# Seven block products over eight row tiles instead of six, with sums left in PSUM, in an encoder layer's feed-forward stages

## The chip, the cores and the metric

The kernel runs on one core of a Trainium2 chip. The metric is device microseconds of one execution, start to end, as the median of several runs. The engines are called as the profile calls them: PE is the matrix engine (PEld its weight loads), DVE the vector engine, ACT the scalar engine, POOL GpSimd, and SP the engine whose queue issues every transfer of this kernel. SBUF is the on-chip memory, PSUM the eight banks into which PE accumulates; one bank holds 128 x 512 float32 numbers.

## What is computed

One encoder layer over 256 tokens of width 2048, in float32. Every sub-layer stands between two RMS norms.

```python
def _swiglu(u, w_gate, w_up, w_down):
    return (jax.nn.silu(u @ w_gate) * (u @ w_up)) @ w_down
...
f = _swiglu(_rmsnorm(h, ffn1_pre_g[i]), ffn1_w_gate[i], ffn1_w_up[i], ffn1_w_down[i])
h = h + 0.5 * _rmsnorm(f, ffn1_post_g[i])
m = _mixer(_rmsnorm(h, mix_pre_g[i]), w_qkv[i], na_rpb[i], out_g[i], w_o[i])
h = h + _rmsnorm(m, mix_post_g[i])
f = _swiglu(_rmsnorm(h, ffn2_pre_g[i]), ffn2_w_gate[i], ffn2_w_up[i], ffn2_w_down[i])
h = h + 0.5 * _rmsnorm(f, ffn2_post_g[i])
g = jax.nn.sigmoid(_rmsnorm(h, ple_pre_g[i]) @ w_ple_gate[i])
h = h + _rmsnorm(g * (p[i] @ w_ple_proj[i]), ple_post_g[i])
```

The two feed-forward networks (FFN1 and FFN2) have 5632 hidden columns, that is 11 blocks of 512. They, their gate, up and down products, hold most of the work and are what the change is about. The mixer between them is attention; it is left as it is but for where some of its tiles lie.

## The kernel before

**Products in three passes.** A float32 number x is split into a high part (`hi`, in the engine's reduced float32 type) and the rest (`lo`). A product of two 128-row tiles is then three matmuls into the same PSUM bank: high by high, low by high, high by low (lines 102 to 104 of `mac`). One matmul has 128 tokens as its stationary operand and 512 weight columns streaming through, so 256 tokens are two tiles, `t` = 0 and 1, and the 2048 input columns are 16 row tiles of a weight matrix. ACT makes the weights' high part (`wh`, line 75) and DVE the low part (`wl`, line 76) from the float32 rows that a transfer brought (`raw`), two row tiles per instruction. There are six buffers each for `wh` and `wl`, three for `raw`.

**Block products.** For ten of the eleven blocks of each FFN, `pair_product` computes the gate and the up products together. Both token tiles by both matrices, over six of the sixteen row tiles in two halves of three, form a 2 x 2 by 2 x 2 block product, which is done in seven block products instead of eight (Strassen's scheme in Winograd's form). For that it needs sums of token blocks (`sums`, four of them, made once per FFN by `token_sums`), sums of weight blocks (line 186, `raw_b`), and sums of the results. The seven products go in the order a11, s1, s2, s4, s3, a12, a22; the four that go into a bank of their own (`pair_s`, two banks) are copied or added out of PSUM into SBUF tiles with the tag `part`, and eight vector instructions (lines 186, 232, 233) form the four outputs there. The other ten row tiles of both matrices (`rest`) are multiplied the plain way into four more banks (`pair_v`, `pair_z`, `pair_y`, `pair_x`), between the block products. The first block of each FFN goes the plain way as a whole.

**Groups.** `swiglu` walks over `FF_GROUPS`, (3, 3, 3, 2) blocks. For each block it runs the pair, then `silu` on ACT (`gs`, line 413) and the product with up on DVE (line 456), and puts the transpose of the result into the list `later`. `run_later` empties this list at fixed places of the next pair or of the down product, where PE transposes (`tr`, line 276) and ACT and DVE write the split hidden block (`hid_h` line 282, `hid_l` line 283). After each group the down product of its blocks runs in four column blocks of 512 and is added onto `f` (lines 468 and 470). In the last group this is followed by the gain, the squares for the norm and the residual (`residual`), whose first part is issued in `mid()`, ahead of the last three row tiles of the last down product.

**Order.** The code is written in dataflow form; a scheduler orders the instructions of each engine before the run, and each engine then takes its own in that fixed order. Pools give a tile the buffer that came free first. A buffer of a pool is waited for by whoever wants to write it next: a transfer on SP's queue, ACT's `wh`, or PE's first matmul into a bank.

Of the kernel before, what the change touches and what calls it, by code (L numbers as in the profile page):

```python
# [19 lines left out]
DFF = 5632  # L20
PLE = 256
# [5 lines left out]
FF_GROUPS = (3, 3, 3, 2)  # L27
# [6 lines left out]
def encoder_layer(ctx: ExitStack, tc: tile.TileContext, a: dict, out: bass.AP):  # L34
# [55 lines left out]
    def mac(acc, xs, parts, first=False, last=False, low_last=False):  # L90


        if low_last:
            for i, ((xh, xl), (wh, wl)) in enumerate(zip(xs, parts)):
                nc.tensor.matmul(acc, xh, wh, start=first and i == 0, stop=False)
                nc.tensor.matmul(acc, xh, wl, start=False, stop=False)
            for i, ((xh, xl), (wh, wl)) in enumerate(zip(xs, parts)):
                nc.tensor.matmul(acc, xl, wh, start=False, stop=last and i == len(parts) - 1)
            return
        for i, ((xh, xl), (wh, wl)) in enumerate(zip(xs, parts)):  # L100
            lead, tail = first and i == 0, last and i == len(parts) - 1
            nc.tensor.matmul(acc, xh, wh, start=lead, stop=False)  # L102
            nc.tensor.matmul(acc, xl, wh, start=False, stop=False)  # L103
            nc.tensor.matmul(acc, xh, wl, start=False, stop=tail)  # L104
# [5 lines left out]
    later, raw_loads, splits, ffn_pool = [], [], [], [None]  # L110
# [48 lines left out]
    def pair_product(lhs, sums, wa, ca, wb, cb):  # L159

        rows1, rows2 = ([lhs[k] for k in ks] for ks in ((0, 1, 4), (2, 3, 5)))
        a11, a12, a22 = of_tile(rows1, 0), of_tile(rows2, 0), of_tile(rows2, 1)
        s1, s2, s3, s4 = sums
        nk = len(lhs)

        def bank(x):
            if x == "s":
                return ps_o.tile([P, NB], F32, name="pair_s", tag="o")
            return ps_acc.tile([P, NB], F32, name=f"pair_{x}", tag="acc")  # L180

        def part(name):
            return ffn_pool[0].tile([P, NB], F32, name=name, tag="part", bufs=6)

        def add(out_, x, y):
            nc.vector.tensor_tensor(out_, x, y, op=ALU.add)  # L186

        def rest(w, k, n, c, accs_, first=False, last=False):

            parts = load_parts(w, k * P, n, c)  # L190
            for t, acc in accs_:
                mac(acc, of_tile(lhs[k : k + n], t), parts, first=first, last=last)

        def load_blocks(w, c):

            raw = ffn_pool[0].tile([P, 2, 3, NB], F32, name="raw_b", bufs=2)
            for j in range(2):
                rows_ = w[2 * j * P : 2 * (j + 1) * P, c : c + NB]
                raw_loads.append(nc.sync.dma_start(raw[:, j, :2], rows_.rearrange("(k p) n -> p k n", p=P)))
                nc.sync.dma_start(raw[:, j, 2], w[(4 + j) * P : (5 + j) * P, c : c + NB])  # L200
            return raw[:, 0], raw[:, 1]

        def split3(raw):
            return split(raw[:, :2]) + split(raw[:, 2:])

        ra1, ra2 = load_blocks(wa, ca)
        rb1, rb2 = load_blocks(wb, cb)
        x = bank("s")
        mac(x, a11, split3(ra1), first=True, last=True)
        p1 = part("p1")  # L210
        nc.scalar.copy(p1, x)
        add(ra1, ra1, rb1)
        x = bank("s")
        mac(x, s1, split3(ra1), first=True, last=True)
        r5 = part("r5")
        nc.scalar.copy(r5, x)
        v, z = bank("v"), bank("z")
        rest(wb, 8, 4, cb, [(1, v), (0, z)], first=True)
        run_later()
        add(ra1, ra1, rb2)  # L220
        x = bank("s")
        mac(x, s2, split3(ra1), first=True, last=True)
        w_ = part("w")
        add(w_, x, p1)
        mac(z, s4, split3(rb2))
        add(rb2, rb1, rb2)
        rest(wb, 12, 4, cb, [(1, v), (0, z)])
        x = bank("s")
        mac(x, s3, split3(rb2), first=True, last=True)
        v_ = part("v")  # L230
        add(v_, x, w_)
        nc.vector.tensor_tensor(w_, r5, w_, op=ALU.subtract)
        nc.vector.tensor_tensor(r5, r5, v_, op=ALU.subtract)
        y, x = bank("y"), bank("x")
        mac(y, a12, split3(ra2), first=True)
        add(ra1, ra1, ra2)
        rest(wb, 6, 2, cb, [(1, v), (0, z)], last=True)
        add(r5, v, r5)
        add(w_, z, w_)
        mac(x, a22, split3(ra1), first=True)  # L240
        for k, n in ((6, 2), (8, 4), (12, 4)):
            rest(wa, k, n, ca, [(0, y), (1, x)], last=k == 12)
        assert nk == 16
        add(p1, y, p1)
        add(v_, x, v_)
        return (p1, v_), (w_, r5)
# [39 lines left out]
    def token_sums(*parts):  # L286


        n_all = sum(p_[0].shape[1] for p_ in parts)
        hi, lo = (  # L290
            acts.tile([P, 2, 2, n_all, P], F32R, name=f"sums_{x}", tag=f"sums_{x}") for x in "hl"
        )
        k0 = 0
        for a11, a12, a21, a22 in parts:
            n = a11.shape[1]
            y = [work.tile([P, 2, 2, P], F32, name="y_s", tag="sq")[:, :, :n] for _ in range(2)]
            nc.vector.tensor_tensor(y[0][:, 0], a21, a22, op=ALU.subtract)
            nc.vector.tensor_tensor(y[0][:, 1], y[0][:, 0], a11, op=ALU.subtract)
            nc.vector.tensor_tensor(y[1][:, 0], a11, a21, op=ALU.subtract)
            nc.vector.tensor_tensor(y[1][:, 1], a12, y[0][:, 1], op=ALU.add)  # L300
            for i in range(2):
                hi_, lo_ = (x[:, i, :, k0 : k0 + n] for x in (hi, lo))
                nc.scalar.copy(hi_, y[i])
                nc.vector.tensor_tensor(lo_, y[i], hi_.bitcast(F32), op=ALU.subtract)
# [30 lines left out]
    def load_x(k):  # L335
# [3 lines left out]
        if k < 6:  # L339
            xb = ffn_pool[0].tile([P, 2, S], F32, name="xb", tag="part", bufs=6)  # L340
        else:
            xb = work.tile([P, 2, S], F32, name="xb", tag="hg")
# [7 lines left out]
        if k < 6:  # L350
            x_first.append(xb)
# [16 lines left out]
    def residual(fg, ssf, scale, blocks, rs, g, sums=None, y_pool=None):  # L368
# [22 lines left out]
        if sums is not None:  # L391
            b0, b1 = y0[::2], y0[1::2]
            later.append(
                lambda: sums.extend(
                    token_sums(
                        [y[:, i : i + 2] for y in b0 for i in (0, 2)],
                        [y[:, i : i + 1] for y in b1 for i in (0, 1)],
                    )
                )
            )  # L400
# [5 lines left out]
    def swiglu(pool, f, ssf, res, blocks, rs, sums, w_gate, w_up, w_down, g_post):  # L406
# [9 lines left out]
        for gi, ng in enumerate(FF_GROUPS):  # L416
            hid = []
            for nb in range(f0, f0 + ng):
# [4 lines left out]
                else:  # L423
                    gate, up = accs("gate"), accs("up")
                    if rs is None:
# [6 lines left out]
                        def ahead_up(k):  # L432
                            load_h(k)
                            if k == KB:
                                with tc.issue_after(splits[0].ins), tc.issue_after(splits[1].ins):
                                    for i, x in enumerate(x_first):
                                        g = row_g[:, 0, 2 * i : 2 * i + 2].unsqueeze(2).broadcast_to([P, 2, S])
                                        nc.vector.tensor_tensor(x, x, g, op=ALU.mult)
                                    a1, a2, a3 = x_first
                                    half = [slice(t * P, (t + 1) * P) for t in range(NT)]  # L440
                                    sums[:] = token_sums(
                                        [x[:, :, h_] for h_ in half for x in (a1, a2)],
                                        [a3[:, i : i + 1, h_] for h_ in half for i in range(2)],
# [9 lines left out]
                split_ = new_split(pool, "hid", 3)  # L453
                for t in range(NT):
                    y = up[t] if nb > 0 else pool.tile([P, NB], F32, name="hm", tag="part", bufs=6)
                    nc.vector.scalar_tensor_tensor(y, up[t], rs[t], gs[t], op0=ALU.mult, op1=ALU.mult)
# [31 lines left out]
    with tc.tile_pool(name="ffn1", bufs=2) as pool:  # L488
        f = pool.tile([P, NT, D], F32, name="f", bufs=1)
        ssf, u_blocks, u_rs = square_sums(), [], []  # L490
# [11 lines left out]
    with ExitStack() as att:  # L502
# [66 lines left out]
        def attend(qT, kT, v, bias, o_split, g):  # L569

            for t in range(NT):
# [46 lines left out]
                on = work.tile([P, KB, HD], F32, name="on", tag="hg")  # L618
# [39 lines left out]
    lhs = rows(o_blocks)  # L658
    pool2 = mix.enter_context(tc.tile_pool(name="mix_f", bufs=1))
    f = pool2.tile([P, NT, D], F32, name="f")  # L660
# [29 lines left out]
    ffn2 = ctx.enter_context(ExitStack())  # L690
    f_pool = ffn2.enter_context(tc.tile_pool(name="f2", bufs=1, side="right"))
    p_h = work.tile([P, PLE // P, S], F32R, name="p_h", tag="hg")
    p_l = work.tile([P, PLE // P, S], F32R, name="p_l", tag="hg")
    with tc.tile_pool(name="ffn2", bufs=2) as pool:
        pT = pool.tile([P, PLE // P, S], F32, name="pT", tag="part", bufs=6)
# [125 lines left out]
```

## Time and profile before

| | |
|---|---|
| median of 3 runs | 1956.0 us (1953.11 to 1956.64) |
| span of the profiled execution | 1954.7 us |
| PE busy | 1930.9 us, 99% |
| DVE busy | 1417.7 us, 73% |
| ACT busy | 1027.5 us, 53% |
| transfers | 376.95 MB, mean 193 GB/s |

The page gives no time of the profiled execution besides its span, from the first to the last instruction; the median of the runs is 1.3 us longer. Busy time is the union of the recorded times of an engine's instructions. A line of a group of instructions reads: line, engine, operation, output<-inputs, shapes, count | busy us, mean ns of one | idle time of the engine just before them, and what ended it. A line of the timeline reads: start us, duration us, engine, line, operation, names, shapes, count [idle time before <-what ended it]. A line of a window reads: start:end length, then busy us and count of PE, PEld, DVE, ACT and POOL, the granted clock of PE, the share of the transfer engines and GB/s.

### The profile page before, as it was taken

How to read it: one execution, taken by the hardware profiler on the slowest of the kernel's cores; microseconds unless marked ns; L12 is line 12 of the kernel's file. 1: busy time of each engine (PE TensorE's matmuls, PEld its weight loads, DVE VectorE, ACT ScalarE, POOL GpSimd, SP SyncE). 2: the span in 40 equal slices, each digit the busy share in tenths (PEclk: the TensorE clock that was granted, in tenths of full speed). 3: DMA queues.
4: the chain of work that ended last, by engine and by line, in shares of the span. 5: the costliest groups of instructions: out<-in, count | busy, mean ns of one | idle time of the engine just before them, and what ended most of it. 6: DMA issues, size and time to landing. Idle time of an engine off the chain costs nothing.

```text
span 1954.7 us, 23225 instructions
## 1 busy us (share of the span) xinstructions
PE 1930.9 (99%) x8780; PEld 1596.7 (82%) x8780; DVE 1417.7 (73%) x1613; ACT 1027.5 (53%) x1320; POOL 22.2 (1%) x31
## 2 busy tenths in 40 slices
PE   8999999999999999999999999999999999999998
PEld 6888888888888877888888878888888888888786
DVE  6984887589759775656565588748975997587864
ACT  7554565355535555544445466545553555355563
POOL 0000000000000000000000000000000000000000
PEclk9999999999999999999999999999999999999999
DMA  9475447445745646454554555744574547456463
GB/s 367 182 248 183 173 176 262 165 173 183 258 162 174 218 158 210 147 197 132 168 175 172 195 210 176 263 164 173 183 259 162 174 181 277 144 183 215 154 207 113
DMA packets 192224, 376.95 MB, mean 193 GB/s; under 512 B 8304, under 2 KB 11376, under 8 KB 191856
## 3 DMA queue, kind: packets, MB, share of 16 engines
q1 hardware_dynamic: 192112, 375.46, 55.4%
q8 instruction: 69, 1.13, 0.2%
q14 instruction: 43, 0.35, 0.1%
HBM read 373.33 MB, written 2.10 MB: 192 GB/s over the span
## 4 chain that ended last, share of the span: by engine, by line
PE 95%; DVE 2%; DMA 1%; ACT 1%; issue 1%; POOL 0%; SPq 0%; DVEq 0%; POOLq 0%; ACTq 0%
PE down L102 8%; PE down L104 8%; PE down L103 8%; PE pair_z L104 3%; PE pair_x L104 3%; PE pair_y L104 3%; PE pair_y L102 3%; PE pair_x L102 3%; PE pair_z L103 3%; PE pair_x L103 3%; PE pair_y L103 3%; PE pair_z L102 3%; PE pair_s L103 3%; PE pair_s L102 3%; PE pair_s L104 3%; PE pair_v L104 2%
## 5 line engine op out<-in xcount | busy, mean ns | idle before, releaser
L76 DVE TENSOR_TENSOR wl<-raw,wh 128x1024 fp32r<-128x1024 f32 (+1 forms) x573 | 693.0, 1220 | 301.1 <-ACT wh L75 282.2
L75 ACT CAST wh<-raw 128x1024 fp32r<-128x1024 f32 (+1 forms) x573 | 596.1, 1051 | 542.1 <-PE down L103 139.4
L75 ACT CAST wh<-raw_b 128x1024 fp32r<-128x1024 f32 (+1 forms) x280 | 228.4, 837 | 139.9 <-PE pair_x L103 55.4
L76 DVE TENSOR_TENSOR wl<-raw_b,wh 128x1024 fp32r<-128x1024 f32 (+1 forms) x280 | 252.0, 953 | 59.4 <-ACT wh L75 58.5
L102 PE MATMUL down<-wh,hid_h 128*128 128x512 f32 x704 | 274.7, 391 | 0.2
L104 PE MATMUL down<-wl,hid_h 128*128 128x512 f32 x704 | 274.0, 389 | 0.0
L103 PE MATMUL down<-wh,hid_l 128*128 128x512 f32 x704 | 273.9, 389 | 0.0
L102 PEld LDWEIGHTS down<-wh,hid_h 128*128 128x128 f32 x704 | 132.1, 188 | 28.1 <-ACT hid_h L282 1.1
L104 PEld LDWEIGHTS down<-wl,hid_h 128*128 128x128 f32 x704 | 132.1, 188 | 27.5
L103 PEld LDWEIGHTS down<-wh,hid_l 128*128 128x128 f32 x704 | 132.2, 188 | 27.2
L186 DVE TENSOR_TENSOR raw_b<-raw_b 128x1536 f32<-128x1536 f32 x80 | 138.8, 1755 | 1.4
L102 PE MATMUL pair_y<-wh,u_h 128*128 128x512 f32 x260 | 101.1, 389 | 0.0
L103 PE MATMUL pair_y<-wh,u_l 128*128 128x512 f32 x260 | 101.1, 389 | 0.0
L104 PE MATMUL pair_y<-wl,u_h 128*128 128x512 f32 x260 | 101.1, 389 | 0.0
L102 PE MATMUL pair_x<-wh,u_h 128*128 128x512 f32 x260 | 101.1, 389 | 0.0
L103 PE MATMUL pair_x<-wh,u_l 128*128 128x512 f32 x260 | 101.1, 389 | 0.0
L104 PE MATMUL pair_x<-wl,u_h 128*128 128x512 f32 x260 | 101.1, 389 | 0.0
L104 PE MATMUL pair_v<-wl,u_h 128*128 128x512 f32 x200 | 77.9, 390 | 0.1
L104 PE MATMUL pair_z<-wl,u_h 128*128 128x512 f32 x200 | 77.9, 389 | 0.0
L103 PE MATMUL pair_v<-wh,u_l 128*128 128x512 f32 x200 | 77.8, 389 | 0.0
L102 PE MATMUL pair_v<-wh,u_h 128*128 128x512 f32 x200 | 77.8, 389 | 0.0
L103 PE MATMUL pair_z<-wh,u_l 128*128 128x512 f32 x200 | 77.8, 389 | 0.0
(234 smaller groups left out, 3314.2 us busy)
## 6 DMA issues: line engine op xcount, KB each, us to landing
raw<-in_ffn_w_down SPq DMA_DIRECT2D x88, 1024.0 KB, 5.0
raw<-in_ffn_w_up SPq DMA_DIRECT2D x48, 1024.0 KB, 8.7
raw<-in_w_qkv SPq DMA_DIRECT2D x48, 1024.0 KB, 5.1
raw<-in_ffn_w_gate SPq DMA_DIRECT2D x47, 1024.0 KB, 5.2
raw_b<-in_ffn_w_gate SPq DMA_DIRECT2D x40, 512.0 KB, 5.9
raw_b<-in_ffn_w_up SPq DMA_DIRECT2D x40, 512.0 KB, 6.7
raw<-in_w_o SPq DMA_DIRECT2D x16, 1024.0 KB, 4.9
raw<-in_w_ple_gate SPq DMA_DIRECT2D x16, 1024.0 KB, 5.0
```

What stands on the lines that cost most here:

```text
L75: nc.scalar.copy(wh[:, :n], raw),
L76: nc.vector.tensor_tensor(wl[:, :n], raw, wh[:, :n].bitcast(F32), op=ALU.subtract),
L102: nc.tensor.matmul(acc, xh, wh, start=lead, stop=False)
L103: nc.tensor.matmul(acc, xl, wh, start=False, stop=False)
L104: nc.tensor.matmul(acc, xh, wl, start=False, stop=tail)
L186: nc.vector.tensor_tensor(out_, x, y, op=ALU.add)
```

## The change

The block products now take eight row tiles in two halves of four. All weights of a pair are then split in units of two row tiles. Three of the seven products (a11, then s2, s3 and a22) go one after the other into the same bank `g1` without clearing it: its value is copied or used after each of the first three, and the next product is added onto it. The up outputs go likewise through `u0`. Thus four PSUM banks are used instead of six, three results are copied out by ACT instead of two, four vector instructions form the outputs instead of eight, and `gate` of token tile 1 is read by `silu` straight from PSUM. The groups become (2, 2, 2, 2, 2, 1), with the two buffers per hidden part that this needs instead of three; the group of one block empties the list `later` before its down product. Tiles move: the token sums into the FFN pools, `part` has four buffers instead of six, `raw_b` has four of four row tiles instead of two of six, and some small tiles change pool. `skip_group_check` on the matmuls only silences a check when the program is built.

```diff
+FF_GROUPS = (2, 2, 2, 2, 2, 1)
-FF_GROUPS = (3, 3, 3, 2)
...
     def pair_product(lhs, sums, wa, ca, wb, cb):
-        rows1, rows2 = ([lhs[k] for k in ks] for ks in ((0, 1, 4), (2, 3, 5)))
-        a11, a12, a22 = of_tile(rows1, 0), of_tile(rows2, 0), of_tile(rows2, 1)
+        k1, k2 = slice(0, KB), slice(KB, 2 * KB)
+        a11, a12, a22 = of_tile(lhs[k1], 0), of_tile(lhs[k2], 0), of_tile(lhs[k2], 1)
...
+        def bank(name):
+            return ps_acc.tile([P, NB], F32, name=f"pair_{name}", tag="acc")
+        def kept(name, x):
+            t = ffn_pool[0].tile([P, NB], F32, name=name, tag="part", bufs=4)
+            nc.scalar.copy(t, x)
+            return t
+        def blocks(w, k, c):
+            raw = ffn_pool[0].tile([P, KB, NB], F32, name="raw_b", bufs=4)
+            rows_ = w[k * P : (k + KB) * P, c : c + NB]
+            raw_loads.append(nc.sync.dma_start(raw, rows_.rearrange("(k p) n -> p k n", p=P)))
+            return raw
...
+        ra1, rb1 = blocks(wa, 0, ca), blocks(wb, 0, cb)
+        rb2 = blocks(wb, KB, cb)
+        g1, u0 = bank("g1"), bank("u0")
+        mac(g1, a11, split4(ra1), first=True, last=True)
+        g0_ = kept("g0_s", g1)
         add(ra1, ra1, rb1)
+        mac(u0, s1, split4(ra1), first=True, last=True)
+        u1_ = kept("u1_s", u0)
         run_later()
         add(ra1, ra1, rb2)
+        mac(g1, s2, split4(ra1), last=True)
+        u0_ = kept("u0_s", g1)
+        u1 = bank("u1")
+        rest(wb, 2 * KB, cb, [(1, u1, True), (0, u0, False)])
+        mac(u0, s4, split4(rb2))
         add(rb2, rb1, rb2)
+        ra2 = blocks(wa, KB, ca)
+        rest(wb, 3 * KB, cb, [(1, u1, False), (0, u0, False)], last=True)
+        add(u0_, u0, u0_, ALU.subtract)
+        mac(g1, s3, split4(rb2), last=True)
+        add(u1_, u1_, g1, ALU.subtract)
+        add(u1_, u1, u1_)
+        g0 = bank("g0")
+        mac(g0, a12, split4(ra2), first=True)
         add(ra1, ra1, ra2)
+        mac(g1, a22, split4(ra1))
+        for k in (2 * KB, 3 * KB):
+            rest(wa, k, ca, [(0, g0, False), (1, g1, False)], last=k == 3 * KB)
+        add(g0_, g0, g0_)
+        return (g0_, g1), (u0_, u1_)
...
-                split_ = new_split(pool, "hid", 3)
+                split_ = new_split(pool, "hid", 2)
...
             hrows = rows(hid)
+            if ng == 1:
+                run_later()
             for b in range(D // NB):
-                gp = gain(pool, g_post, b * NB, "g_post", "part", 6) if last else None
+                gp = gain(pool, g_post, b * NB, "g_post", "part", 4) if last else None
```

`token_sums` is called with two parts of two row tiles each per half instead of one of two and one of one, and at the start of FFN1 four pieces of x instead of three are scaled for it. The mixer's `f` and the second set of sums lie in a pool `f2` that is opened before the mixer's output product.

More of the change, by code (lines that the diff above doesn't have):

```diff
@@ L108, in of_tile @@
         return [(hi[:, tok], lo[:, tok]) for hi, lo in lhs]
-    later, raw_loads, splits, ffn_pool = [], [], [], [None]
+    later, raw_loads, splits, ffn_pool, sums_pool = [], [], [], [None], [None]
     def product(
@@ L182, in part @@
[L182 to L201, printed above, removed]
@@ L203, in split3 @@
-        def split3(raw):
-            return split(raw[:, :2]) + split(raw[:, 2:])
[L206 to L211, printed above, removed]
-        add(ra1, ra1, rb1)
[L213 to L217, printed above, removed]
@@ new lines, in split4, with add, rest @@
+        def split4(raw):
+            return split(raw[:, :2]) + split(raw[:, 2:])
+        def add(out_, x, y, op=ALU.add):
+            nc.vector.tensor_tensor(out_, x, y, op=op)
+        def rest(w, k, c, accs_, last=False):
+            parts = load_parts(w, k * P, KB, c)
+            for t, acc, lead in accs_:
+                mac(acc, of_tile(lhs[k : k + KB], t), parts, first=lead, last=last)
+        ra1, rb1 = blocks(wa, 0, ca), blocks(wb, 0, cb)
+        rb2 = blocks(wb, KB, cb)
+        g1, u0 = bank("g1"), bank("u0")
@@ L229, in pair_product @@
[L229 to L235, printed above, removed]
-        add(ra1, ra1, ra2)
[L237 to L242, printed above, removed]
@@ L290, in token_sums @@
         hi, lo = (
-            acts.tile([P, 2, 2, n_all, P], F32R, name=f"sums_{x}", tag=f"sums_{x}") for x in "hl"
+            sums_pool[0].tile([P, 2, 2, n_all, P], F32R, name=f"sums_{x}", tag=f"sums_{x}", bufs=1) for x in "hl"
         )
@@ L349, in load_x @@
             )
-        if k < 6:
+        if k < 2 * KB:
             x_first.append(xb)
@@ L391, in residual @@
         if sums is not None:
-            b0, b1 = y0[::2], y0[1::2]
             later.append(
[L394 to L399, printed above, removed]
+                lambda: sums.extend(token_sums(*([y[:, i : i + 2] for y in y0] for i in (0, 2))))
             )
@@ L452, in swiglu @@
                         gs = [gated(gate[t], t) for t in range(NT)]
-                split_ = new_split(pool, "hid", 3)
+                split_ = new_split(pool, "hid", 2)
                 for t in range(NT):
-                    y = up[t] if nb > 0 else pool.tile([P, NB], F32, name="hm", tag="part", bufs=6)
+                    y = up[t] if nb > 0 else pool.tile([P, NB], F32, name="hm", tag="part", bufs=4)
                     nc.vector.scalar_tensor_tensor(y, up[t], rs[t], gs[t], op0=ALU.mult, op1=ALU.mult)
@@ L687, in encoder_layer @@
     mix.close()
[L690 to L693, printed above, removed]
+    p_h = f_pool.tile([P, PLE // P, S], F32R, name="p_h")
+    p_l = f_pool.tile([P, PLE // P, S], F32R, name="p_l")
     with tc.tile_pool(name="ffn2", bufs=2) as pool:
-        pT = pool.tile([P, PLE // P, S], F32, name="pT", tag="part", bufs=6)
+        pT = pool.tile([P, PLE // P, S], F32, name="pT", tag="part", bufs=4)
         nc.sync.dma_start(pT, a["pT"].rearrange("(k p) s -> p k s", p=P))
```

41 lines of the change are left out of this document (13 added, 28 removed).

## The prediction, made before the changed kernel was run

> **What bounds the kernel now.** I read the page's busy lines and its slices first, then the timeline of PE, then windows cut at the pairs and the down products, and last the groups and waits of one pair.
>
> ```profile
> span 1954.7 us, 23225 instructions
> ...
> PE 1930.9 (99%) x8780; PEld 1596.7 (82%) x8780; DVE 1417.7 (73%) x1613; ACT 1027.5 (53%) x1320; POOL 22.2 (1%) x31
> ...
> PEclk9999999999999999999999999999999999999999
> ```
>
> PE is never idle for long and its clock is granted in full; all its gaps together are 1954.7 - 1930.9 = 23.8 us. What one matmul costs is read from the starts, since the records overlap:
>
> ```profile
> 672.00 0.39 PE L102 MATMUL pair_x<-wh,u_h 128*128 128x512 f32 x1
> 672.23 0.39 PE L103 MATMUL pair_x<-wh,u_l 128*128 128x512 f32 x1
> 672.45 0.39 PE L104 MATMUL pair_x<-wl,u_h 128*128 128x512 f32 x1
> ```
>
> A matmul is recorded with 0.39 us, but the next one starts 0.227 us later. The windows bear this out (first a pair without transposes, then one with eight, a down product of three blocks, and FFN1's last down product of two):
>
> ```profile
> 204.03:245.51 41.48, 41.48 (x185) 34.35 (x183) 36.26 (x37) 23.20 (x28) 0.00 (x0) 1.00 0.58 203
> 245.51:287.88 42.37, 42.37 (x192) 35.17 (x191) 38.14 (x41) 24.61 (x31) 0.00 (x0) 1.00 0.55 199
> ...
> 330.25:396.43 66.18, 66.18 (x298) 54.88 (x296) 37.60 (x37) 26.15 (x27) 0.00 (x0) 1.00 0.51 175
> 672.68:718.94 46.26, 46.04 (x210) 37.52 (x209) 32.54 (x41) 23.46 (x34) 0.55 (x1) 1.00 0.55 182
> ```
>
> 183 weight loads in 41.48 us are 0.2267 us each: the pair runs at PE's pace with no gap at all. DVE is busy 38.14 of 42.37 us (90%) in a full pair, against 57% in a down product. So PE is the bound, with DVE close behind it in the pairs alone.
>
> **What the change removes: three matmuls a pair.** Before: seven products x 3 row tiles x 3 passes = 63, and ten plain row tiles x 2 matrices x 2 token tiles x 3 = 120: 183, the count above. After: 7 x 4 x 3 = 84 and 8 x 2 x 2 x 3 = 96: 180. Twenty pairs save 60 matmuls; 60 x 0.2267 = **13.6 us**, wholly on the path. By the recorded 0.39 us it would be 23 us. [...]
>
> **What it adds to DVE and ACT in a pair.** From the groups of the pair at 245.51, DVE and then ACT:
>
> ```profile
> L76 DVE TENSOR_TENSOR wl<-raw,wh 128x1024 fp32r<-128x1024 f32 x10 | 12.1, 1219 | 1.6 <-ACT wh L75 1.6
> L76 DVE TENSOR_TENSOR wl<-raw_b,wh 128x1024 fp32r<-128x1024 f32 x7 | 8.5, 1221 | 1.8 <-ACT wh L75 1.8
> L186 DVE TENSOR_TENSOR raw_b<-raw_b 128x1536 f32<-128x1536 f32 x4 | 6.9, 1755 | 0.1
> L76 DVE TENSOR_TENSOR wl<-raw_b,wh 128x512 fp32r<-128x512 f32 x7 | 4.8, 685 | 0.0
> ...
> L186 DVE TENSOR_TENSOR v<-pair_x,v 128x512 f32<-128x512 f32 x1 | 0.7, 684 | 0.0
> ```
>
> ```profile
> L75 ACT CAST wh<-raw_b 128x1024 fp32r<-128x1024 f32 x7 | 7.4, 1054 | 4.8 <-PE pair_x L103 3.5 <-PE pair_z L103 0.8 <-ACT hid_h L282 0.3
> L75 ACT CAST wh<-raw_b 128x512 fp32r<-128x512 f32 x7 | 4.3, 621 | 2.0 <-PE pair_x L103 1.7 <-PE pair_s L103 0.3
> ...
> L216 ACT COPY r<-pair_s 128x512 f32<-128x512 f32 x1 | 0.6, 582 | 0.0
> ```
>
> DVE now: 17 x 1.22 + 7 x 0.685 = 25.5 for the splits, 4 x 1.755 = 7.0 for the weight sums, 8 x 0.684 = 5.5 for the outputs: 38.0 us. After: 22 splits x 1.22 = 26.8; four weight sums over 2048 columns, at 1.755 + (1.755 - 0.684) / 2 = 2.29 us each by the step from 512 to 1536 columns, 9.2; four outputs, 2.7: 38.7 us. So DVE gains 0.7 us a pair and reaches 38.8 of 41.7 us, 93%. ACT: 17 x 1.05 + 7 x 0.62 + 2 x 0.58 = 23.4 becomes 22 x 1.05 + 3 x 0.58 = 24.8, at about 26 of 41.7 us. I cost both at nothing, because the waits of this pair show slack:
>
> ```profile
> ACT wh L75 <- PE pair_z L103: 5.6, 5, 3.1
> ACT wh L75 <- PE pair_x L103: 5.2, 3, 3.5
> DVE wl L76 <- ACT wh L75: 3.4, 4, 1.6
> ```
>
> ACT waits for PE to give back `wh` buffers, 10.8 us in a pair, and DVE for ACT: the splits run ahead of PE as far as six buffers allow. The cover is DVE's 4.2 us of idle time a pair, of which 1.4 us go (0.7 of work, 0.7 of PE time); if it were gone, each further DVE microsecond would be one of the span's. Groups of two give DVE a down product after two pairs instead of three.
>
> **What it adds as waits inside a pair.** `g1` is read and then added onto, which no bank of the kernel before is. PE's next product into it waits for the reader. After a11 and s2 the reader is an ACT copy (0.58 us), with s1's 12 x 0.2267 = 2.7 us, and much more, between. After s3 it is one DVE subtraction (0.68 us) with only a12's 2.7 us between. Cost: nothing if DVE comes to it within 2.0 us; if it has to finish a weight sum (2.29) and a split (1.22) first, 2.29 + 1.22 + 0.68 - 2.72 = 1.5 us a pair, 29 us in all. Below nothing it can't be, since PE has no gap here. I take nothing, nearer to the rows above where DVE waits for others. [...] Between pairs I see no wait: the pool gives the bank that came free first, so the next `g1` is the old `u0`, and `silu` reading the old `g1` delays only what needs the fourth bank. SP issues four transfers of 1 MB for the blocks instead of eight smaller ones, and the bytes are the same; `ra2` now comes after others on SP's queue but is needed late. Next pair's `ra1` takes `rb1`'s buffer, free in mid-pair.
>
> **What it adds at the groups' ends.** A group of two has its second block's transposes after the first half of the first down step:
>
> ```profile
> 678.56 0.60 PE L276 MATMUL tr<-ident,r 128*128 128x128 f32 x4
> 678.92 0.48 PE L102 MATMUL down<-wh,hid_h 128*128 128x512 f32 x1
> 679.23 0.40 PE L103 MATMUL down<-wh,hid_l 128*128 128x512 f32 x1
> 679.73 0.50 PE L102 MATMUL down<-wh,hid_h 128*128 128x512 f32 x1
> ```
>
> Here PE lost 0.50 - 0.23 = 0.27 us. There are two such starts now and ten after: 8 x 0.27 = **2.2 us** (0 to 5, if ACT is later). The group of one has nothing to do but wait. What leads to its first down matmul is seen at the end of FFN1's last pair, whose last matmul starts at 672.45, on ACT and on DVE:
>
> ```profile
> 672.71 1.06 ACT L75 CAST wh<-raw 128x1024 fp32r<-128x1024 f32 x1 [0.15 <-PE pair_x L103]
> 674.45 0.73 ACT L413 ACTIVATE gs<-v,r 128x512 f32<-128x512 f32 x1 [0.68 <-DVE v L186]
> ```
>
> ```profile
> 673.73 0.68 DVE L186 TENSOR_TENSOR v<-pair_x,v 128x512 f32<-128x512 f32 x1
> 674.33 1.21 DVE L76 TENSOR_TENSOR wl<-raw,wh 128x1024 fp32r<-128x1024 f32 x1
> 675.46 0.74 DVE L456 SCALAR_TENSOR_TENSOR r<-r,r,gs 128x512 f32<-128x512 f32 x1
> ```
>
> After: matmuls end at about 672.9; the cast that stands first on ACT ends at 673.8; silu 0.73, product 0.74, then transposes at about 675.3; PE has idled from 672.7 but for tile 0's transposes, 0.5 us. That is 2.1 us, less what PE may put in between; without the cast, 1.3. I take **2.0** for each FFN, 4.0 (2.6 to 5.4).
>
> **What it takes from the tail of an FFN.** The last down product's tail needs cover for the norm:
>
> ```profile
> 711.85 0.39 PE L104 MATMUL down<-wl,hid_h 128*128 128x512 f32 x1
> ...
> 715.25 0.39 PE L104 MATMUL down<-wl,hid_h 128*128 128x512 f32 x1
> 715.67 1.34 PE L276 MATMUL tr<-ident,h 128*128 128x128 f32 x8
> ```
>
> Tile 0 ends at 711.85; PE runs 15 of tile 1's 24 matmuls, and the residual's first transposes come just as these end. With one block tile 1 has 12 in all: PE has 12 x 0.2267 = 2.7 us less to do while DVE's chain runs. Either the whole 2.7 us shows, or nothing, if tile 1's own chain starts as much earlier. I take half, **1.4** for each FFN, 2.8 (0 to 5.4). In this product DVE has, for each 5.44 us of PE (24 matmuls), two splits and four instructions of 0.68: 5.2 us. It keeps up but no more. The gains wait on SP for `part` buffers, ahead of weights.
>
> **Elsewhere.** Adding onto `f` happens five times instead of three per column block and FFN: 32 more DVE instructions of 0.68, in down products where DVE is 57% busy: hidden. The token sums grow (rows of FFN1's start):
>
> ```profile
> L438 DVE TENSOR_TENSOR xb<-xb,row_g 128x512 f32<-128x512 f32 x3 | 1.9, 686 | 0.0
> L304 DVE TENSOR_TENSOR sums_l<-y_s,sums_h 128x512 fp32r<-128x512 f32 x2 | 1.3, 689 | 0.2 <-ACT sums_h L303 0.2
> L304 DVE TENSOR_TENSOR sums_l<-y_s,sums_h 128x256 fp32r<-128x256 f32 x2 | 0.8, 418 | 0.0
> ...
> L299 DVE TENSOR_TENSOR y_s<-xb 128x256 f32<-128x256 f32 x1 | 0.4, 418 | 0.0
> L299 DVE TENSOR_TENSOR y_s<-xb 128x128 f32<-128x128 f32 x1 | 0.3, 285 | 0.0
> ```
>
> One `xb` (0.69), 2 x 0.27 and 4 x 0.13: 1.8 us of DVE in FFN1 and 1.1 in FFN2, ahead of a plain up product; I take **0.3** (0 to 2.9). Tiles that only change pool cost nothing unless a transfer waits for the new place.
>
> **The sum**, against the profiled execution: -13.6 + 2.2 + 4.0 + 2.8 + 0.3 = -4.3 us, so a span of 1950.4 us; against the median, 1.3 us longer than that span, **1951.7 us**. With all edges low it is -13.6 + 2.6 = -11.0 (1945.0), with all high -13.6 + 5 + 5.4 + 5.4 + 2.9 = +5.1 (1961.1).
>
> **Rivals.** (1) The edges are nearly free, because PE's order is filled with other ready work: about -10 us, 1946. For it speaks that PE lost only 0.27 us at 679; against it, that one block leaves nothing else ready. (2) Slower: DVE comes late to the subtraction after s3. The point is 8.2 / 20 = 0.41 us a pair, from which the time is 3.9 us above before; at half of the worst price, 0.75 us, it is 15 us, 1966.7. For it speaks DVE's 93% and its two weight sums close to each other there; against it, the waits above, all of them on PE's buffers. (3) The products are saved but the wait and the edges just eat it: 0.2 us a pair more, 1955.7, no change.
>
> **How the numbers follow.** Differences under 0.2%, 3.9 us, are about what this measurement can't tell from none. The main case has 0.58, its own range 1947 to 1956; about six parts in ten of it lie below 1952.1. Rival 1 has 0.13, rival 2 0.20, rival 3 0.09. Faster: 0.35 + 0.13 = 0.48; slower 0.20 and 0.02 of the main case; the rest, 0.30, the same. The range goes from 1944.5 to 1963, which leaves out little of rival 1 and the upper half of rival 2.
>
> **What would show it.** 180 matmuls a pair with 0.227 us between starts, a pair of about 40.8 us without and 41.7 with transposes; no wait of PE on the DVE subtraction of `g1`; DVE at 93% of a pair; a gap of some 2 us ahead of the first down matmul of the last group and 0.3 us at each group of two. Wrong would make it: gaps in every pair at a22 or s2, PE waiting for `wl` in the second pair of a group, or a longer tail between the FFNs and what follows.

## The result and the profile after

The changed kernel takes **1971.7 us** (median of 4 runs, 1970.4 to 1972.8) against 1954.8 for the kernel before in the same session: the ratio of the runs is 1.0081, 95% interval 1.0068 to 1.0095 (the two medians alone give 1.0086). It is 0.8% slower, where 1951.7 and a gain were forecast; the time lies above the range. The page of the changed kernel:

```profile
span 1969.0 us, 22703 instructions
...
PE 1931.5 (98%) x8720; PEld 1587.8 (81%) x8720; DVE 1464.4 (74%) x1526; ACT 1052.9 (53%) x1300; POOL 22.2 (1%) x31
...
L183 DVE TENSOR_TENSOR raw_b<-raw_b 128x2048 f32<-128x2048 f32 x80 | 183.0, 2288 | 1.4
```

PE has the 60 matmuls less (8720 for 8780), and its busy time is as long as before: it counts the slower matmuls that are shown below at their full length (recorded with 0.63 us instead of 0.39), so the saving doesn't show in it. The span is 14.3 us longer than the 1954.7 of before. Where the time lies is seen from the two kernels cut at the same places: start and first block, first pair of FFN1, rest of FFN1, mixer and plain block of FFN2, rest of FFN2, and what follows. The columns are the window, its length, the busy times of PE, PEld, DVE, ACT and POOL, the granted clock, the share of DMA and GB/s. First before, then after:

```profile
0.00:52.67 52.67, 46.08 (x192) 37.00 (x193) 36.69 (x57) 36.72 (x63) 1.86 (x9) 1.00 0.94 350
52.67:95.48 42.81, 42.67 (x192) 35.10 (x191) 40.13 (x42) 24.77 (x31) 0.00 (x0) 1.00 0.54 197
95.48:718.94 623.46, 623.24 (x2793) 516.25 (x2792) 471.86 (x488) 327.09 (x385) 0.55 (x1) 1.00 0.56 195
718.94:1173.86 454.92, 450.12 (x2170) 372.62 (x2168) 290.06 (x416) 230.27 (x343) 15.57 (x15) 1.00 0.52 177
1173.86:1839.69 665.83, 665.61 (x2984) 551.42 (x2982) 508.96 (x525) 351.34 (x414) 0.55 (x1) 1.00 0.56 194
1839.69:1954.70 115.01, 103.13 (x457) 84.30 (x455) 70.00 (x89) 57.32 (x90) 3.66 (x5) 0.96 0.48 165
```

```profile
0.00:53.28 53.28, 46.58 (x192) 36.90 (x193) 35.26 (x55) 36.06 (x60) 1.86 (x9) 1.00 0.97 359
53.28:103.71 50.43, 45.99 (x189) 36.69 (x188) 42.38 (x38) 27.82 (x31) 0.00 (x0) 0.93 0.57 205
103.71:732.07 628.36, 621.24 (x2765) 511.14 (x2763) 498.19 (x454) 338.34 (x377) 1.46 (x1) 1.00 0.55 192
732.07:1182.54 450.47, 449.26 (x2168) 373.39 (x2169) 287.69 (x413) 230.20 (x340) 13.76 (x15) 1.00 0.52 178
1182.54:1848.54 666.00, 663.45 (x2946) 544.18 (x2945) 528.84 (x477) 362.42 (x402) 0.00 (x0) 1.00 0.55 193
1848.54:1969.00 120.46, 105.02 (x465) 85.46 (x463) 72.08 (x94) 58.01 (x92) 5.13 (x6) 0.94 0.43 148
```

The differences are +0.6, **+7.6**, +4.9 and -4.4 (together +0.5, since a wait at the mixer's start moved ahead of it), +0.2 and **+5.4** us. So the first pair and what follows FFN2 lost 13 us, and the two long stretches, in which 6.1 and 6.8 us of matmuls were saved, gained nothing.

**The first pair of FFN1.** PE's rows at its second product, s1:

```profile
58.81 0.50 PE L102 MATMUL pair_u<-wh,sums_h 128*128 128x512 f32 x1 [1.77 <-ACT wh L75]
59.15 0.39 PE L103 MATMUL pair_u<-wh,sums_l 128*128 128x512 f32 x1
60.07 0.71 PE L104 MATMUL pair_u<-wl,sums_h 128*128 128x512 f32 x1 [0.53 <-DVE wl L76]
60.58 0.63 PE L102 MATMUL pair_u<-wh,sums_h 128*128 128x512 f32 x1
61.01 0.63 PE L103 MATMUL pair_u<-wh,sums_l 128*128 128x512 f32 x1
```

PE stands still for 1.77 us ahead of s1, for 0.53 until `wl` is there, and then matmuls start 0.43 us apart, not 0.227. The same comes again ahead of s2 (at 65.84 and 67.10). In numbers: 1.81 + 0.69 + 1.79 + 0.70 = 5.0 us of waits, and some 3.4 us in matmuls at half rate. Why nothing was ready is in the rows of ACT and DVE:

```profile
47.54 0.62 ACT L243 ACTIVATE sq<-h 128x512 f32<-128x512 f32 x1
...
49.56 1.27 ACT L381 ACTIVATE gs<-gate,r 128x512 f32<-128x512 f32 x2
50.72 2.00 ACT L75 CAST wh<-raw_b 128x1024 fp32r<-128x1024 f32 x2
56.21 0.59 ACT L170 COPY g_s<-pair_g 128x512 f32<-128x512 f32 x1 [3.49 <-PE pair_g L104]
57.71 1.99 ACT L75 CAST wh<-raw_b 128x1024 fp32r<-128x1024 f32 x2 [0.92 <-DVE raw_b L183]
```

```profile
55.40 2.28 DVE L183 TENSOR_TENSOR raw_b<-raw_b 128x2048 f32<-128x2048 f32 x1
58.79 2.36 DVE L76 TENSOR_TENSOR wl<-raw_b,wh 128x1024 fp32r<-128x1024 f32 x2 [1.11 <-ACT wh L75]
```

ACT comes to the pair's first cast only at 50.72, after the squares of `h` and the silu of the first block, 2.5 us before PE needs it. From there a11, s1 and s2 follow each other on the same buffer `ra1`: weight sum (2.28), cast, split, product, weight sum again. Weight sum and first cast alone (2.28 + 1.05) take longer than the 2.7 us of matmuls of the product ahead of them. Before, 24 plain up matmuls lay between s1 and s2.

That explains the wait ahead of s2. The one ahead of s1 has another cause, since s1 follows a11 at once in the kernel before, too. There the same work was done earlier, the first cast 6.3 us and the weight sum 3.3 us ahead of the pair's start at 52.67:

```profile
46.39 1.04 ACT L75 CAST wh<-raw_b 128x1024 fp32r<-128x1024 f32 x1
```

```profile
49.33 1.76 DVE L186 TENSOR_TENSOR raw_b<-raw_b 128x1536 f32<-128x1536 f32 x1
```

In the changed kernel ACT is through with the squares of `h` only at 48.25 us, before at 44.50. Which part of the change put them back is not shown by a run.

**What follows FFN2.** The residual's transposes wait longest, before and after:

```profile
1846.79 1.29 PE L276 MATMUL tr<-ident,h 128*128 128x128 f32 x8 [1.49 <-DVE h L381]
```

```profile
1861.24 1.51 PE L250 MATMUL tr<-ident,h 128*128 128x128 f32 x6 [5.43 <-DVE h L355]
```

After this wait, too, matmuls and transposes run at half rate (0.43 and 0.21 us), from 1859.02 to 1865.84 us; in the kernel before from 1849.04 to 1852.46.

**Inside the steady pairs** PE waits at none of the four products that go through `g1` (a11, s2, s3 and a22): there is no gap at a22 or after the subtraction. A group of two pairs takes, in FFN1 and FFN2:

```profile
403.80:486.60 82.80, 82.79 (x370) 68.32 (x368) 74.87 (x66) 51.37 (x56) 0.00 (x0) 1.00 0.62 223
1397.62:1480.91 83.29, 83.29 (x370) 68.29 (x368) 74.96 (x66) 51.38 (x56) 0.00 (x0) 1.00 0.62 221
```

PE's own pace would be 360 x 0.2267 + 8 x 0.107 (a transpose) = 82.5 us. The 0.107 is an estimate, half of the 0.213 us between the starts of transposes at half rate (1861.48 to 1862.76); at full rate their starts are 0.109 us apart (the median of the trace), 0.02 us more for eight. FFN1 loses 0.3 a group, in one wait for `wl`; FFN2 loses 0.8, and there the matmuls on the token sums start 0.23 to 0.24 us apart:

```profile
1574.12 0.40 PE L102 MATMUL pair_g<-wh,sums_h 128*128 128x512 f32 x1
1574.35 0.40 PE L103 MATMUL pair_g<-wh,sums_l 128*128 128x512 f32 x1
1574.59 0.39 PE L104 MATMUL pair_g<-wl,sums_h 128*128 128x512 f32 x1
1574.82 0.40 PE L102 MATMUL pair_g<-wh,sums_h 128*128 128x512 f32 x1
```

### The profile page after: what moved, and what is told of

It is laid out like the page before. It is cut to its first block, busy times and chain, and to the rows that moved or that the text cites. A ratio compares the mean times of both kernels' runs of the same rounds, so it can differ in the third digit from the quotient of the medians.

```text
span 1969.0 us, 22703 instructions
## 1 busy us (share of the span) xinstructions
PE 1931.5 (98%) x8720; PEld 1587.8 (81%) x8720; DVE 1464.4 (74%) x1526; ACT 1052.9 (53%) x1300; POOL 22.2 (1%) x31
## 4 chain that ended last, share of the span: by engine, by line
PE 94%; DVE 2%; ACT 2%; issue 1%; DMA 1%; POOL 0%; DVEq 0%; POOLq 0%; SPq 0%; ACTq 0%
PE pair_g L104 8%; PE pair_g L103 8%; PE pair_g L102 8%; PE down L102 8%; PE down L103 8%; PE down L104 8%; PE pair_u L104 6%; PE pair_u L102 6%; PE pair_u L103 6%; PE v L104 1%; PE v L102 1%; PE v L103 1%; PE mo L103 1%; PE mo L102 1%; PE mo L104 1%; ACT wh L75 1%
## 5 line engine op out<-in xcount | busy, mean ns | idle before, releaser
L75 ACT CAST wh<-raw_b 128x1024 fp32r<-128x1024 f32 x280 | 287.1, 1053 | 257.9 <-DVE raw_b L183 136.4
L76 DVE TENSOR_TENSOR wl<-raw_b,wh 128x1024 fp32r<-128x1024 f32 x280 | 332.6, 1221 | 65.8 <-ACT wh L75 62.1
L104 PE MATMUL pair_g<-wl,u_h 128*128 128x512 f32 x560 | 217.9, 389 | 0.0
L102 PE MATMUL pair_g<-wh,u_h 128*128 128x512 f32 x560 | 217.8, 389 | 0.0
L103 PE MATMUL pair_g<-wh,u_l 128*128 128x512 f32 x560 | 217.8, 389 | 0.0
L183 DVE TENSOR_TENSOR raw_b<-raw_b 128x2048 f32<-128x2048 f32 x80 | 183.0, 2288 | 1.4
L104 PE MATMUL pair_u<-wl,u_h 128*128 128x512 f32 x320 | 125.9, 393 | 0.1
L102 PE MATMUL pair_u<-wh,u_h 128*128 128x512 f32 x320 | 124.6, 389 | 0.0
L103 PE MATMUL pair_u<-wh,u_l 128*128 128x512 f32 x320 | 124.5, 389 | 0.0
L102 PEld LDWEIGHTS pair_g<-wh,u_h 128*128 128x128 f32 x560 | 105.1, 188 | 22.0
```

The lines of the kernel that those rows point to most:

```text
L75: nc.scalar.copy(wh[:, :n], raw),
L76: nc.vector.tensor_tensor(wl[:, :n], raw, wh[:, :n].bitcast(F32), op=ALU.subtract),
L102: nc.tensor.matmul(acc, xh, wh, start=lead, stop=False, skip_group_check=True)
L103: nc.tensor.matmul(acc, xl, wh, start=False, stop=False, skip_group_check=True)
L104: nc.tensor.matmul(acc, xh, wl, start=False, stop=tail, skip_group_check=True)
L183: nc.vector.tensor_tensor(out_, x, y, op=op)
```

## The experiments

Theory after the result: the pair product brings its matmuls, and the loss comes from where it was put: (a) the order a11, s1, s2 where nothing is split ahead (the first pair of FFN1), (b) the one-block group at the end, (c) PE's half rate after idle time, (d) the sums' new place in memory. The rival is the prediction's own: DVE, at 90% of a pair, is too late. Each ratio below is to the kernel before, run beside the version; its median was between 1954.8 and 1956.5 us, so a difference in us between two versions is good to some 2 us.

**The group of one first, or fifth, not last.**

```
-FF_GROUPS = (2, 2, 2, 2, 2, 1)
+FF_GROUPS = (1, 2, 2, 2, 2, 2)     one_first
+FF_GROUPS = (2, 2, 2, 2, 1, 2)     one_fifth
```

> The changed kernel with groups (1, 2, 2, 2, 2, 2): the single block is the first, plain one, and the last down product has two blocks again. Theory (the loss is at the edges: FFN1's first pair meets no work done ahead and its three products on one sum chain show, and a one-block last down product leaves the norm's chain uncovered): FFN1's first pair falls from 50.4 to about 42 us (-8), the gap of 4.1 us and the half-rate matmuls behind FFN1's last down product go (-5), FFN2's tail gives back 5; the one-block starts keep their 2.4 us at another place. Together about -17: 1954 us, ratio to before 1.000. Rival A (the chain a11, s1, s2 shows in the first pair whatever stands before it): 50.4 stays, about 1962, ratio 1.004. Rival B (the pairs themselves are the slow part): about 1968 to 1972, ratio 1.007.

> The changed kernel with groups (2, 2, 2, 2, 1, 2): the last down product has two blocks again, the single block stands fifth, FFN1's first pair still comes right after the plain block. Theory: the tails give back about 10 us, FFN1's first pair stays at 50 us: 1962 us, ratio 1.0035. Rival (the tail is slow for another reason, such as where tiles lie or the order of the residual): 1970 to 1972, ratio 1.008, with the gap of 4 us behind FFN1's last down product still there.

One block first: 1955.2 us, ratio to the kernel before 0.9995 (0.9986 to 1.0005): 16.5 us less than the changed kernel, from one line. The first group of pairs then comes after a down product and loses nothing (first row), and the wait ahead of the residual's transposes after FFN2 falls from 5.43 to 1.34 us (second):

```profile
81.50:163.99 82.49, 82.49 (x370) 68.39 (x368) 72.34 (x64) 51.69 (x57) 0.00 (x0) 1.00 0.64 223
```

```profile
1850.94 1.29 PE L250 MATMUL tr<-ident,h 128*128 128x128 f32 x8 [1.34 <-DVE h L355]
```

One block fifth: 1967.3 us, 1.0053 (1.0038 to 1.0068). The first pair stays at 50.39, and FFN2's end is as good as before (17.3 us for the product that follows FFN2, 18.1 in the kernel before, 23.0 with one block last). It gains only 4.4 us of the 9.7 expected. In its trace each of the two one-block starts is followed by 3.4 us at half rate (from 575.74 and 1698.72), so that their down products take 24.8 and 24.7 us; in the changed kernel's trace neither is, and FFN2's takes 23.1. And at the start of the mixer a wait of 2.3 us for `wl` is there again (at 748.45), which the kernel before has too (2.8 us, at 740.11); the changed kernel waits 3.9 us for the residual instead, at 729.55, and not there. So (a) and (b) are both real, and (b) shows at FFN2's end and hardly at FFN1's.

**The new groups without the new product.**

```
 # the kernel before
-FF_GROUPS = (3, 3, 3, 2)
+FF_GROUPS = (2, 2, 2, 2, 2, 1)
+            if ng == 1:
+                run_later()
```

> The kernel before, its block products over six row tiles untouched, with the groups (2, 2, 2, 2, 2, 1) and the list emptied ahead of a one-block down product. Theory: tails cost about 10 us, one-block starts 4.8, eight more two-block starts 2.2, FFN1's first pair stays near 43 us as its order has plain work between s1 and s2: about 1970 us, ratio 1.008, although nothing of the pairs is changed. Rival (the new pairs carry the loss): 1957 to 1960, ratio 1.002.

1969.8 us, 1.0067 (1.0052 to 1.0082). The groups alone lose 13.7 us against the kernel before of the same session, with the old pairs unchanged at 41.48 and 42.37 and the first at 42.9. In these groups the new product gains nothing (1.0081 against 1.0067, overlapping), where it should take 13.6 us.

**The plain up blocks between s1 and s2 again.**

```
         u1_ = kept("u1_s", u0)
+        u1 = bank("u1")
+        rest(wb, 2 * KB, cb, [(1, u1, True), (0, u0, False)])
         run_later()
         add(ra1, ra1, rb2)
         mac(g1, s2, split4(ra1), last=True)
         u0_ = kept("u0_s", g1)
-        u1 = bank("u1")
-        rest(wb, 2 * KB, cb, [(1, u1, True), (0, u0, False)])
```

> The changed kernel with one step moved: the first plain load of the up matrix and its 24 matmuls come between the products s1 and s2, as in the order of the kernel before, not behind s2. Theory (chain of weight sum, cast and split of one buffer shows where nothing independent lies between two products): in FFN1's first pair the gap of 2.0 us ahead of s2 and its half-rate matmuls go, the one ahead of s1 stays; that pair falls from 50.4 to about 46 us, the time to 1967, ratio 1.006; the steady pairs stay at 82.8 us for two. Rival (the gap is from the late start of the pair's first split alone): the gap moves on to the plain load and 50 us stay.

1965.5 us, 1.0046 (1.0031 to 1.0061), 6.3 less than the changed kernel. The first pair takes 46.48. The wait for `wh` ahead of s2 is gone (0.53 us for `wl` stay); the one ahead of s1 is left, in this trace without half rate after it:

```profile
52.83:99.31 46.48, 43.69 (x190) 34.09 (x189) 41.31 (x37) 27.03 (x30) 0.00 (x0) 1.00 0.60 210
```

FFN1's groups fall to 82.49, PE's own pace; FFN2's to 83.12. So the 0.3 us for `wl` in the steady groups was the order, too.

**PE's idle time filled in the first pair**, by 8 matmuls ahead of s1 (into `u0`) and 8 ahead of s2 (into `u1`).

```
+        def fill(acc, parts):
+            for i in range(8 if first_pair[0] else 0):
+                nc.tensor.matmul(acc, a11[i % 4][0], parts[i % 4][0], start=True, stop=True, ...)
...
+        fill(u0, parts)
...
+        fill(u1, parts)
```

> The changed kernel with 8 extra matmuls (of 227 ns, into a bank that is started afresh afterwards, from operands of the block product before) ahead of s1 and again ahead of s2, in the first pair of the first feed-forward alone: TensorE has work in the two stretches of 2.04 and 2.02 us in which it stood idle there. The order of the splits is the same. Theory: of the 7.6 us that this pair lost, some 3.5 are the matmuls that start 427 ns apart after the two gaps (about 17 of them, 0.2 each too long), and the half rate comes from the idle time; with the gaps filled the matmuls stay at 227, the pair falls from 50.4 to about 47 us and the whole by about 3.5, though 16 matmuls more are run. Rival: the half rate has nothing to do with the idle time (the weights' place, or the transfers at that time); then the 427s stay and the pair stays at 50.4 or a little over.

The pair takes 47.1 us with 16 matmuls more in it, and the granted clock of the stretch from 58 to 71 us is full, where the changed kernel has 0.74. The changed kernel, then this one:

```profile
58.00:71.00 13.00, 9.52 (x24) 6.67 (x25) 10.94 (x10) 7.99 (x10) 0.00 (x0) 0.74 0.00 1
```

```profile
53.39:100.49 47.10, 46.19 (x206) 37.36 (x204) 41.18 (x37) 28.22 (x31) 0.00 (x0) 1.00 0.61 216
58.00:71.00 13.00, 12.09 (x55) 9.30 (x55) 12.48 (x12) 10.27 (x13) 0.00 (x0) 1.00 0.07 12
```

So (c) is shown: the half rate came from the idle time, and cost 3.3 us here. The whole gained less, 1969.6 us, 1.0069 (1.0054 to 1.0084), which overlaps the changed kernel's interval: in the traced execution matmuls ran at half rate after the one-block start of FFN1 (0.427 us apart from 701.31 to 704.29), which they don't in the changed kernel's.

**The token sums in the old pool.**

```
-            sums_pool[0].tile([P, 2, 2, n_all, P], F32R, ..., bufs=1) for x in "hl"
+            acts.tile([P, 2, 2, n_all, P], F32R, ..., bufs=1) for x in "hl"
```

> The changed kernel with the token sums of both feed-forwards in the pool acts again, as in the kernel before, in place of the pools of the feed-forwards. In the second feed-forward of the changed kernel a group of two pairs takes 83.27 us, 0.5 over the first feed-forward's 82.80, and the matmuls on the sums start 231 to 235 ns apart there, where the others start 227 apart. Theory A: it is the place of the sums in memory that sets this; then the sums' matmuls go back to 227, the five groups of the second feed-forward fall to at most 82.8 each, and the whole is 2 to 3 us below the changed kernel (about 1969). Rival B: the cadence belongs to the second feed-forward for another reason (what else reads or writes at that time); then the groups stay at 83.27 and the whole at 1971.7.

The FFN2 groups go to FFN1's time, and the sums' matmuls to 0.227 us:

```profile
1396.67:1479.47 82.80, 82.78 (x369) 68.31 (x368) 74.85 (x66) 51.35 (x56) 0.00 (x0) 1.00 0.63 224
```

```profile
1572.45 0.39 PE L102 MATMUL pair_g<-wh,sums_h 128*128 128x512 f32 x1
1572.67 0.39 PE L103 MATMUL pair_g<-wh,sums_l 128*128 128x512 f32 x1
1572.90 0.39 PE L104 MATMUL pair_g<-wl,sums_h 128*128 128x512 f32 x1
```

So (d) is shown: 0.5 us a group, 2 us in all FFN2 pairs. The whole is at 1969.8, 1.0074 (1.0059 to 1.0089), its interval overlapping that of the changed kernel; in the traced execution 1.6 us of the gain were lost to half rate after FFN2's one-block start. What about the place does it (another buffer beside it, or the address) stays open.

**More work for DVE.**

```
         add(rb2, rb1, rb2)
+        add(rb1, rb1, rb1)
```

> The changed kernel with one more VectorE instruction per pair: rb1 is doubled onto itself after its last use, 2.29 us on VectorE in each of 20 pairs, with no reader of the result; nothing else changes. It measures the cover that VectorE has in a pair of the changed kernel (busy 37.4 of 41.4 us). If the work of a pair is bound by TensorE with 4 us to spare in the pair, the steady groups stay at 82.8 and 83.3 and the whole is within 3 us of 1971.7. If VectorE's order is already the limit at some stage of the pair, each pair is longer by up to 2.29 us, 46 us in all. Between: if the cover is there on average but not at the place, the wait ahead of the next stage lengthens by 0.5 to 1 us a pair, 10 to 20 us.

1975.5 us, 1.0103 (1.0086 to 1.0120), about 4 us more for 46 us more DVE work; the interval overlaps the changed kernel's. A group of two pairs in FFN1 takes 83.17 for 82.80; in FFN2 it stays at 83.29:

```profile
404.96:488.13 83.17, 83.10 (x369) 68.25 (x368) 77.49 (x66) 49.09 (x55) 0.00 (x0) 1.00 0.61 211
```

The prediction's slower rival falls: at 93% DVE still costs next to nothing, 0.4 us for two pairs, and the down products between them stay at 44.83 us.

**Three blocks in the last down product, in the kernel before.**

```
-FF_GROUPS = (3, 3, 3, 2)
+FF_GROUPS = (2, 3, 3, 3)
```

> The kernel before with groups (2, 3, 3, 3) in place of (3, 3, 3, 2): the same pairs and blocks, with three blocks in the last down product and two in the first. The tail's stall of the kernel before (3.17 us at 740, where TensorE waits on the na_bias product) comes ahead of a product bound by VectorE; if a longer last product gives VectorE the time to get ahead, the first feed-forward's end is 2 to 4 us shorter and the second's 1 to 2, the whole 1951 to 1955. If the stalls at the end depend only on the work after the last product, nothing changes: 1956.

1956.1 us, 1.0007 (0.9998 to 1.0016): nothing. Two blocks in the last product are enough; it is the step from two to one that costs.

**The versions put together.** Three edits of the changed kernel at once (the block of one first, the plain up blocks between s1 and s2, the sums in `acts`); the same groups without the new product; and the new product in groups none of which has one block:

```
FF_GROUPS = (1, 2, 2, 2, 2, 2)   one_first_rest_acts: + up blocks between s1 and s2, sums in acts
FF_GROUPS = (1, 2, 2, 2, 2, 2)   before_one_first: the kernel before, + run_later()
FF_GROUPS = (2, 2, 2, 2, 3)      rest_acts_22223: as the first, hid bufs=3, raw_b bufs=3
```

> Three edits of the changed kernel at once: groups (1, 2, 2, 2, 2, 2), the plain up blocks between s1 and s2 again, and the token sums in acts. If the three effects are separate and add: from the 1955.2 of the groups alone, less 0.3 for each of the steady groups of the first feed-forward (1.3), less 0.15 to 0.7 for each of the second's (0.7 to 3): 1950 to 1953, just under the kernel before at 1956. If the last product of two blocks is bound by VectorE whatever comes ahead of it, a saving ahead of it is given back there, as in the group variant with the one block in fifth place, where the first feed-forward's last down product stalled again; then 1955 as with the groups alone.

> The kernel before with groups (1, 2, 2, 2, 2, 2) and the jobs of the one-block group run as in the changed kernel: the new group sizes, in the better order, without the new pair product. With one_first_rest_acts (1951.7, the same groups with the new pair product) it gives what the pair product alone is worth. By the rows, two pairs take 83.85 us before and 82.49 there, ten times: 13.6, so about 1964 to 1965 here; if the pairs of before are shorter where VectorE is not behind (41.48 in place of 42.37), down to 1956.

> The changed kernel with groups (2, 2, 2, 2, 3), so no group of one block at all and three blocks in the last down product, with the plain up blocks between s1 and s2 again and the sums in acts (hid gets a third buffer, raw_b one less). Against one_first_rest_acts (1951.7) it saves the start of the one-block group (about 3 us in the first feed-forward, 2 in the second) and one group start, and gets the first pair beside the transfers of the start again (46.5 in place of 41.2, 5 us). If both hold, 1951 to 1953: the two orders are worth the same. If the smaller raw_b ring holds back the loads, each pair is longer by up to 1 us and the whole is up to 20 us longer.

one_first_rest_acts takes 1951.7 us, 0.9979 (0.9970 to 0.9989); before_one_first 1962.1, 1.0034 (1.0022 to 1.0045). With the same groups the new product is worth 0.55%, 10.8 us, and two pairs take, without it in before_one_first and with it in rest_acts_22223:

```profile
77.99:161.84 83.85, 83.85 (x375) 69.52 (x374) 71.74 (x75) 48.97 (x58) 0.00 (x0) 1.00 0.61 214
```

```profile
145.90:228.39 82.49, 82.49 (x369) 68.40 (x368) 74.54 (x65) 51.99 (x56) 0.00 (x0) 1.00 0.66 223
```

rest_acts_22223 takes **1949.9 us**, 0.9971 (0.9961 to 0.9980), and beats both kernels, though its first pair is at 47.9 us again, with half rate after a wait of 1.84 us. The smaller `raw_b` ring costs nothing (82.49 us for two pairs, PE's own pace). The two put-together versions overlap in their intervals; which is the better isn't settled.

## Why the prediction was wrong

- **60 matmuls, -13.6 us: right.** 82.49 against 83.85 us for two pairs, ten times, is 13.6; the whole shows 10.8 with equal groups.
- **"I cost both at nothing, because the waits of this pair show slack": wrong where it mattered most.** I took the cover from a steady pair, where the splits run ahead of PE, and applied it to all twenty. In the first pair of FFN1 nothing runs ahead. It takes 50.4 us where its pace is 180 x 0.2267 + 8 x 0.107 = 41.7, 8.7 us more, and before lost 0.4 there. I looked at `g1` and its readers and not at the order: that s2 now follows s1 at once, with weight sum, cast and split of the same buffer between. With the old order back the pair falls by 4.0 us, some 1.7 of them because no half rate followed the wait ahead of s1 in that trace. The rest, the wait ahead of s1 above all, comes from ACT's first cast, only 2.5 us ahead of the pair and not 6.3; that is read from the rows and not shown by a run. In the steady pairs of FFN1 the step held but for 0.3 us a group.
- **No term for PE's half rate.** Not in the sum at all; 3.3 us in the first pair, and part of the ends'. I took the clock as granted in full from slices of 49 us, in which it can't be seen: the kernel before has stretches of 3.4 us at half rate, too, from 739.71 and from 1849.04, each at a wait.
- **Two-block starts, 8 x 0.27: too small.** A down product of two blocks takes 44.83 us for 192 x 0.2267 + 8 x 0.107 = 44.4, so 0.45 us is lost in each of ten; less what the kernel before lost at such places, 3.8 us.
- **One-block starts, 2.0 each: nearly right.** FFN1's, with the 1.59 and 0.45 us that PE waits:

```profile
702.36 0.50 PE L102 MATMUL down<-wh,hid_h 128*128 128x512 f32 x1 [1.59 <-ACT hid_h L256]
703.31 0.52 PE L250 MATMUL tr<-ident,u_s 128*128 128x128 f32 x3 [0.45 <-DVE u_s L422]
```

  By the starts PE comes 1.75 and 0.72 us late, 2.5 us in each FFN, 4.9 in all. The cause is the one forecast, silu, product and transposes.
- **FFN tails, 1.4 each: mis-sized.** Half of the missing cover was a guess between two ends. Beyond PE's pace, and without the one-block start, the end of FFN1 with the mixer lost 0.7 us against before, because the wait of 2.8 us for `wl` that follows there in the kernel before went as well. The end of FFN2 lost 4.1, as nothing follows that could give it back: the wait ahead of the transposes grew from 1.49 to 5.43 us, by more than the 2.7 us that I had as the worst case, and the half rate lasted 6.8 us and not 3.4.
- **"Tiles that only change pool cost nothing": wrong**, by 0.5 us a group in FFN2, 2 us in all. I looked for a transfer that waits, and it was the matmuls that read them.
- **The slower rival** (the subtraction after s3) gave the nearest time, 1966.7, by the wrong mechanism: PE waits nowhere there, DVE is at 90% of a pair and not 93%, and 46 us more DVE work cost about 4. The eaten-up rival named the kind of cause, waits and edges against the products, with amounts far too small.

Counted in both kernels as time beyond PE's pace (0.2267 us a matmul, 0.107 a transpose), the terms are -13.6 + 3.8 (two-block starts) + 4.9 (one-block starts) + 4.8 (tails) + 8.3 (first pair) + 1.5 and 4.0 (the other pairs of FFN1 and FFN2) + 0.6 (start) = 14.3 us, the whole difference of the spans.

## What to carry to other kernels

A cover read from a steady iteration says nothing on the first one: go through the new order of stages once for the iteration in which nothing is prepared, and ask of each product what must be done on the other engines between its predecessor and it. A change that comes as a bundle (a better product, other groups, other pools) can be right in its main part and lose all of it to the rest; here the product was worth 10.8 us and the groups alone cost 13.7. A short remainder belongs where work follows it and not at the end of a chain.

## What the runs showed of the hardware

**Half rate after a window of 3.4 us in which PE was idle for about half of it.** In the first pair matmuls start 0.427 us apart from about 60.2 to 63.6 us, then at full rate, and again from about 67.0 to 70.4. The granted clock changes on a grid: in the changed kernel's trace half rate begins at 60.19, 67.02, 729.21, 1859.02 and 1961.42 us, the last four 2, 196, 527 and 557 times 3.4133 us after the first. In the trace of the kernel before it begins at 739.71, 1849.04 and 1948.03 us, the last two 325 and 354 such steps after the first; in that of `one_fifth` the two beginnings named above, 575.74 and 1698.72, are 329 steps apart. So in these traces it is the idle time within one window of the grid that half rate goes with. Single windows, each with the one after it, first of the changed kernel, then of `rest_between`:

```profile
56.78:60.19 3.41, 1.12 (x6) 0.44 (x5) 2.30 (x3) 2.49 (x5) 0.00 (x0) 1.00 0.02 7
60.19:63.61 3.42, 3.42 (x9) 2.65 (x10) 3.42 (x4) 0.49 (x1) 0.00 (x0) 0.50 0.02 5
63.61:67.02 3.41, 1.34 (x5) 0.47 (x3) 2.14 (x3) 2.76 (x4) 0.00 (x0) 1.00 0.00 0
67.02:70.43 3.41, 3.33 (x8) 2.65 (x9) 3.41 (x5) 2.55 (x3) 0.00 (x0) 0.50 0.00 0
```

```profile
55.55:58.97 3.42, 1.77 (x11) 1.09 (x9) 2.31 (x2) 2.43 (x3) 0.00 (x0) 1.00 0.02 7
58.97:62.38 3.41, 2.89 (x13) 2.39 (x14) 3.41 (x4) 3.31 (x6) 0.00 (x0) 1.00 0.02 5
```

PE is idle for 2.29 and 2.07 us in the changed kernel's two windows at full clock, and half rate follows; for 1.65 us in that of `rest_between`, and the clock stays full. In the traces of the changed kernel and of the kernel before, after the first 20 us, half rate followed all eight windows at full clock with 1.74 us of idle time or more (the 1.74 in the kernel before, 1845.63 to 1849.04) and none of the others, of which the longest idle time is 1.13 us (698.49 to 701.90 in the changed kernel). Where the edge lies between is not known more closely: a matmul's record lasts 0.39 us and the next one starts after 0.227, so an idle time is uncertain by some 0.16 us, an estimate from these two, and the 1.65 and 1.74 us are nearer to each other than that. An idle stretch of the whole window isn't needed here: about half of it did it. The grid fits what the same one-block start of FFN2 (waits of 1.6 and 0.45 us) did in two executions: in that of `sums_in_acts` matmuls start 0.43 us apart after it (1824.96 to 1827.52); in the changed kernel's they don't, and there the edge at 1824.88 splits it into windows with 1.04 and 0.99 us of idle time. It fits, too, that a wait of 1.64 us with 0.53 after it brought no half rate in `rest_between`: the edge of the windows above, at 58.97, lies between the two.

**Where the stationary operand lay changed a matmul's time**: 0.233 us in the changed kernel for 0.227 in `sums_in_acts`, on token sums in one pool of two, the same code otherwise. It was shown by moving them; the reason wasn't. The product after FFN2 (`pp`) fits it: the change moved its `p_h` and `p_l` from `work` into the same pool, `f2`, and its first twelve intervals are 0.233 us each (1848.54 to 1851.34), in the kernel before 0.227 (1839.69 to 1842.41).
